# Three down-projection quarters as seven block products with weight sums built by accumulating transfers

## The chip, the cores and the metric

One core of one Trainium2 chip runs the kernel. The metric is the device time of one launch in microseconds (us), over several runs; lower is better. The kernel before has a median of 1753.64 us over 3 runs (1753.59 to 1753.92).

## What is computed

A two-layer decoder trunk over 512 positions with model width 1024, in float32. Each layer normalizes its input, makes one combined projection, runs four attention-like mixers, mixes them through gates and an output projection, and then runs a feed-forward block. The change touches the feed-forward block alone:

```python
for l in range(DEPTH):                      # DEPTH = 2
    ...
    x = x + mixed @ w_out[l]
    h2 = rmsnorm(x, norm2_g[l])
    x = x + jnp.square(jax.nn.relu(h2 @ w_up[l])) @ w_down[l]
return rmsnorm(x, final_g)
```

Here `w_up` is 1024 x 4096 and `w_down` is 4096 x 1024, so the hidden width is 4096.

## The kernel before

**Split products.** TensorE works on fp32r operands. Each fp32 operand is held as a high half (a copy to fp32r) and a low half (the value less its high half), and each product of a 128x128 stationary block with a 128x512 moving block is made by the three matmuls of `mm3` (L288 to L291): high by high, high by low, low by high.

**The weight stream.** All large weights are stored in one array, in the order in which they are used, in pieces of 128 x 2 x 512 (two blocks of 128 rows of the contraction by 512 columns, 512 KB). `weight_plan` (L62) writes that order. `WeightStream` loads a piece into one of three `raw` buffers by a transfer on SP's queue (L105) and splits it: ScalarE (ACT) writes the high half `whi` (L114), VectorE (DVE) the low half `wlo` (L116). The split halves have three buffers each (`wsp`). `next` hands out a piece and issues the splits of the pieces up to two places ahead of it, so a piece's split can start when the piece three places earlier has been used up.

**A large product.** `big` (L293) makes a 512 x 512 result in four PSUM accumulators (`acc`, a pool of four) over eight blocks of the contraction, in four pieces. In each piece it runs over the four accumulators `m` and the two blocks `q`, with one `mm3` each: 24 matmuls a piece, 96 for the result. `evac` then empties each accumulator.

**The feed-forward block.** `up(b)` (L1022) makes 512 of the 4096 hidden rows by `big`, transposed (hidden rows on partitions, 512 tokens in the free dimension), and its `evac` makes relu (L1027), the square (L1029), the high half `ah` (L1032) on ACT and the low half `al` (L1033) on DVE for each 128 rows. `down(c, half)` (L1038) contracts quarter `c` of the hidden rows (1024 of them, eight blocks) with 512 of the 1024 output columns; its `evac` adds the scaled accumulators to the residual `xs` on DVE (L1041). The two are interleaved: while quarter `c` is contracted, the two `up` products of quarter `c + 1` run, in the order up, down, up, down. The last quarter has no `up` beside it. `r2` is the squared reciprocal norm, which is applied at the `evac` of `down`.

```python
        acts = up(0) + up(1)
        for c in range(4):
            nxt = up(2 * c + 2) if c < 3 else []
            for half in range(2):
                down(c, half, acts, finish if l + 1 == DEPTH and c == 3 and half == 1 else None)
                if half == 0 and c < 3:
                    nxt = nxt + up(2 * c + 3)
```

The order on each engine comes from a scheduling layer, which places instructions by what they depend on; within one engine it is then fixed, and an instruction that waits holds those behind it.

Of the kernel before, what the change touches and what calls it, by code (L numbers as in the profile page):

```python
# [8 lines left out]
F32 = mybir.dt.float32  # L9
F32R = mybir.dt.float32r  # L10
# [6 lines left out]
P = 128  # L17
# [43 lines left out]

def weight_plan():  # L62
    plan = []

    def block(layer, key, kt, n):
        for p in range(0, kt, 2):
            plan.append((layer, key, p, min(2, kt - p), n))

    for l in range(DEPTH):
        for b in ("BA", "BF"):  # L70
            block(l, (b,), KD, BA_N if b == "BA" else 512)
        block(l, ("uq",), 2, 384)
        block(l, ("ukv",), 1, 512)
        for b in ("BV", "BD", "BN"):
            block(l, (b,), KD, 512)
        for br in LIFT_ORDER:
            for half in range(2):
                block(l, ("gate", br, half), KD, 512)
                block(l, ("lift", br, half), 2, 512)
        for half in range(2):  # L80
            block(l, ("out", half), KD, 512)
        block(l, ("up", 0), KD, 512)
        block(l, ("up", 1), KD, 512)
        for c in range(4):
            if c < 3:
                block(l, ("up", 2 * c + 2), KD, 512)
            block(l, ("down", c, 0), KD, 512)
            if c < 3:
                block(l, ("up", 2 * c + 3), KD, 512)
            block(l, ("down", c, 1), KD, 512)  # L90
    return plan


class WeightStream:
    def __init__(self, nc, raw, split, wbig, ahead=W_AHEAD, ahead_raw=AHEAD_RAW):
        self.nc, self.raw, self.split, self.wbig = nc, raw, split, wbig
        self.plan = weight_plan()
        self.ahead, self.ahead_raw = ahead, ahead_raw
        self.pos = self.n_dma = self.n_split = 0
        self.raws, self.parts = {}, {}  # L100

    def _dma(self, j):
        _, _, _, kk, n = self.plan[j]
        t = self.raw.tile([P, 2, 512], F32, name="raw", tag="raw")
        self.nc.sync.dma_start(t[:, :kk, :n], self.wbig[j, :, :kk, :n])  # L105
        self.raws[j] = t

    def _split(self, j):
        _, _, _, kk, n = self.plan[j]
        t = self.raws.pop(j)  # L110
        pool, bufs = (self.last_pool, 1) if j == len(self.plan) - 1 else (self.split, 3)
# [3 lines left out]
        eng = self.nc.gpsimd if self.plan[j][1] in ON_POOL and self.plan[j][2] % 4 else self.nc.vector  # L115
        b = eng.tensor_tensor(  # L116
            lo[:, :kk, :n], t[:, :kk, :n], hi[:, :kk, :n].bitcast(F32), op=ALU.subtract)
        self.parts[j] = (hi, lo)
        return a.ins, b.ins
# [7 lines left out]
    def take(self, what):  # L127

        assert self.plan[self.pos][:3] == what
        self.pos += 1  # L130
        return self.parts.pop(self.pos - 1) + self.plan[self.pos - 1][3:]
# [6 lines left out]
    def prefetch(self):  # L138
        last = len(self.plan)
        while self.n_split < min(self.pos + self.ahead, last):  # L140
            while self.n_dma < min(self.n_split + self.ahead_raw, last):
                self._dma(self.n_dma)
                self.n_dma += 1
# [3 lines left out]
    def next(self, layer, key, p):  # L147
# [4 lines left out]
        return self.parts.pop(j) + self.plan[j][3:]  # L152
# [3 lines left out]
def kernel(  # L156
# [53 lines left out]
    tiny([P, 8], "pad", 1)  # L210
# [77 lines left out]
    def mm3(o, ah, al, bh, bl, start, stop):  # L288
        pe.matmul(o, ah, bh, start=start, stop=False)  # L289
        pe.matmul(o, ah, bl, start=False, stop=False)  # L290
        return pe.matmul(o, al, bh, start=False, stop=stop).ins  # L291
# [155 lines left out]
    for l in range(DEPTH):  # L447
# [574 lines left out]
        def up(b):  # L1022
            res = []

            def evac(m, ps):
                t = xp.tile([P, SEQ], F32, name="relu", tag="relu", bufs=3)
                act.activation(t, ps, AF.Relu)  # L1027
                a = xp.tile([P, SEQ], F32, name="sq", tag="sq", bufs=3)
                act.activation(a, t, AF.Square)  # L1029
                hi = xp.tile([P, SEQ], F32R, name="ah", tag="ah", bufs=16)  # L1030
                lo = xp.tile([P, SEQ], F32R, name="al", tag="al", bufs=16)
                act.activation(hi, a, AF.Copy)  # L1032
                dve.tensor_tensor(lo, a, hi.bitcast(F32), ALU.subtract)  # L1033
                res.append((hi, lo))
            big(l, ("up", b), ht, evac, token_stationary=False)
            return res
# [30 lines left out]
        acts = up(0) + up(1)  # L1067
# [4 lines left out]
        for c in range(4):  # L1072
            nxt = up(2 * c + 2) if c < 3 else []
            for half in range(2):
                down(c, half, acts, finish if l + 1 == DEPTH and c == 3 and half == 1 else None)
                if half == 0 and c < 3:
                    nxt = nxt + up(2 * c + 3)
                if c == 3:
                    if l + 1 < DEPTH:
                        htn += norm_half(xs, half, g1, ssq, xp)  # L1080
                        nc.scalar.dma_start(
                            x_dram[l + 1].rearrange("(m p) d -> p m d", p=P)[:, :, half * 512:(half + 1) * 512],
                            xs[half])
                    elif half == 0:
                        sq_half(xs, half, ssq, xp)
                        for m in range(NT):
                            pool.tensor_tensor(xs[0][:, m, :], xs[0][:, m, :], fg[:, 0:512], op=ALU.mult)
            acts = nxt
# [17 lines left out]
def _pack_weights(np, inp):  # L1106
    plan = weight_plan()
# [66 lines left out]
```

## Time and profile before

| | us |
|---|---|
| median of 3 runs | 1753.64 |
| the profiled execution's own time | 1754.36 |
| span of its profile | 1752.6 |
| TensorE (PE) busy in the span | 1730.7 (99%) |
| PE weight loads (PEld) | 1402.9 (80%) |
| DVE busy | 876.2 (50%) |
| ACT busy | 826.2 (47%) |
| GpSimd (POOL) busy | 137.3 (8%) |

The first feed-forward block runs from 529.3 to 879.6 us of the span, the second one ends the program. A matmul's row in the timeline lasts longer than the distance to the next one, since matmuls are pipelined; what one costs in a stream is read from the distance between starts. The profile also gives the granted clock of TensorE in each stretch (PEclk, 1.00 is full).

### The profile page before, as it was taken

To read this page: it belongs to the slowest core of one execution; us is meant where nothing else is said; L and a number is where in the kernel's file an instruction comes from. 1 tells how busy PE (TensorE), PEld (TensorE's weight loads), DVE (VectorE), ACT (ScalarE), POOL (GpSimd) and SP (SyncE) were. 2 spreads that over 40 slices of the span, in tenths; PEclk is the share of its full clock that TensorE was granted. 3 is DMA by queue.
4 is the path that set the end of the run, shared out by engine and by line. 5 is a ranking of instruction groups with operands and counts; after the bars stand their busy time and mean duration, and the time that the engine had idled before them with its cause. 6 is when DMAs were issued, how large, how long until landed. Compare 5 with 4: busy or idle time off the path is not lost.

```text
span 1752.6 us, 22592 instructions
## 1 busy us (share of the span) xinstructions
PE 1730.7 (99%) x8849; PEld 1402.9 (80%) x8849; DVE 876.2 (50%) x1570; ACT 826.2 (47%) x1525; POOL 137.3 (8%) x153
## 2 busy tenths in 40 slices
PE   9999999999999999999999999999999999999998
PEld 7877777778788888888888777777788888888886
DVE  5445999543443333333344479985434433333333
ACT  7576745572334433333346776365623343333332
POOL 2112001011200000000021110011112000000002
PEclk9999999999999999999999999999999999999999
DMA  4222111112242222333332211211124323223322
GB/s 158 96 65 69 61 61 61 61 61 93 88 134 95 97 96 96 96 97 98 115 112 85 72 61 61 83 43 57 61 96 132 108 86 107 96 97 96 96 96 73
DMA packets 50681, 154.07 MB, mean 88 GB/s; under 512 B 5648, under 2 KB 14352, under 8 KB 50576
## 3 DMA queue, kind: packets, MB, share of 16 engines
q1 hardware_dynamic: 48368, 149.41, 26.2%
q10 hardware_dynamic: 2208, 3.23, 0.5%
q8 instruction: 70, 1.15, 0.3%
q14 instruction: 35, 0.29, 0.1%
HBM read 148.43 MB, written 4.19 MB: 87 GB/s over the span
## 4 chain that ended last, share of the span: by engine, by line
PE 86%; DVE 7%; ACT 4%; issue 1%; POOL 0%; POOLq 0%; DVEq 0%; ACTq 0%
PE acc L289 23%; PE acc L291 23%; PE acc L290 23%; PE T L476 3%; PE O L545 2%; PE S L289 2%; DVE wlo L116 2%; PE S L290 2%; PE S L291 2%; ACT whi L114 1%; DVE sc L788 1%; DVE m L787 1%; PE S L487 1%; PE S L488 1%; DVE sc L805 1%
## 5 line engine op out<-in xcount | busy, mean ns | idle before, releaser
L116 DVE TENSOR_TENSOR wlo<-raw,whi 128x1024 fp32r<-128x1024 f32 (+1 forms) x268 | 338.1, 1261 | 556.3 <-ACT whi L114 555.7
L114 ACT ACTIVATE whi<-raw 128x1024 fp32r<-128x1024 f32 (+1 forms) x268 | 281.7, 1051 | 604.2 <-PE acc L291 377.8
L289 PE MATMUL acc<-whi,hth 128*128 128x512 f32 (+1 forms) x960 | 389.1, 405 | 0.0
L290 PE MATMUL acc<-wlo,hth 128*128 128x512 f32 (+1 forms) x960 | 377.2, 393 | 0.5 <-DVE wlo L116 0.5
L291 PE MATMUL acc<-whi,htl 128*128 128x512 f32 (+1 forms) x960 | 377.0, 394 | 0.0
L291 PEld LDWEIGHTS acc<-whi,htl 128*128 128x128 f32 x960 | 180.6, 188 | 35.4
L289 PEld LDWEIGHTS acc<-whi,hth 128*128 128x128 f32 x960 | 181.2, 189 | 33.3 <-issue 2.7
L290 PEld LDWEIGHTS acc<-wlo,hth 128*128 128x128 f32 x960 | 181.1, 189 | 31.3 <-DVE wlo L116 0.8
L289 PE MATMUL acc<-hth,whi 128*128 128x512 f32 x512 | 199.5, 390 | 0.0
L290 PE MATMUL acc<-wlo,ah 128*128 128x512 f32 x512 | 199.4, 389 | 0.0
L289 PE MATMUL acc<-whi,ah 128*128 128x512 f32 x512 | 199.4, 389 | 0.0
L291 PE MATMUL acc<-whi,al 128*128 128x512 f32 x512 | 199.4, 389 | 0.0
L290 PE MATMUL acc<-htl,whi 128*128 128x512 f32 x512 | 199.3, 389 | 0.0
L291 PE MATMUL acc<-hth,wlo 128*128 128x512 f32 x512 | 199.3, 389 | 0.0
L290 PEld LDWEIGHTS acc<-wlo,ah 128*128 128x128 f32 x512 | 96.1, 188 | 20.4 <-DVE wlo L116 0.4
L290 PEld LDWEIGHTS acc<-htl,whi 128*128 128x128 f32 x512 | 96.1, 188 | 20.0
L291 PEld LDWEIGHTS acc<-hth,wlo 128*128 128x128 f32 x512 | 96.1, 188 | 20.0
L289 PEld LDWEIGHTS acc<-whi,ah 128*128 128x128 f32 x512 | 96.1, 188 | 19.8
L291 PEld LDWEIGHTS acc<-whi,al 128*128 128x128 f32 x512 | 96.1, 188 | 19.8
L289 PEld LDWEIGHTS acc<-hth,whi 128*128 128x128 f32 x512 | 96.1, 188 | 19.7
L520 ACT ACTIVATE PT<-T 128x128 f32<-128x128 f32 (+3 forms) x160 | 69.4, 433 | 62.9 <-PE T L476 61.5
L499 DVE TENSOR_REDUCE nm<-S 128x1 f32<-128x128 f32 (+3 forms) x160 | 77.0, 485 | 39.5 <-PE S L497 27.9
(228 smaller groups left out, 2115.7 us busy)
## 6 DMA issues: line engine op xcount, KB each, us to landing
raw<-in_wbig SPq DMA_DIRECT2D x256, 512.0 KB, 3.3
x<-in_x SPq DMA_DIRECT2D x8, 512.0 KB, 5.9
raw<-in_wbig SPq DMA_DIRECT2D x8, 472.0 KB, 4.7
xmid<-x ACTq DMA_DIRECT2D x2, 1024.0 KB, 4.6
x<-xmid SPq DMA_DIRECT2D x4, 512.0 KB, 5.3
ck<-in_cmpk SPq DMA_DIRECT2D x4, 256.0 KB, 4.2
ck<-in_cmpv SPq DMA_DIRECT2D x4, 256.0 KB, 3.7
out<-o ACTq DMA_DIRECT2D x4, 256.0 KB, 2.8
```

Source lines behind the costliest of these rows:

```text
L114: a = self.nc.scalar.activation(hi[:, :kk, :n], t[:, :kk, :n], AF.Copy)
L116: b = eng.tensor_tensor(lo[:, :kk, :n], t[:, :kk, :n], hi[:, :kk, :n].bitcast(F32), op=ALU.subtract)
L289: pe.matmul(o, ah, bh, start=start, stop=False)
L290: pe.matmul(o, ah, bl, start=False, stop=False)
L291: return pe.matmul(o, al, bh, start=False, stop=stop).ins
L476: pe.transpose(t[:width, m * P:(m + 1) * P], s, ident)
L487: pe.matmul(s[:, :n], q[0][:, qc], k[0][:, :n], start=True, stop=False)
L488: pe.matmul(s[:, :n], q[0][:, qc], k[1][:, :n], start=False, stop=False)
L499: dve.tensor_reduce(nm, s[:, :n], axis=AX.X, op=ALU.max, negate=True)
L520: act.activation(pT[:, :n], t[:, :n], AF.Copy)
L545: pe.matmul(o[64 * e:64 * e + 64, P * i:P * (i + 1)], paths[c][2](j, h + e), pTs[e][:, j * P:(j + 1) * P], start=(j == 0 and c == 0 and ex ...
L787: dve.max(m8, a[:, :n])
```

## The change

The first three of the four quarters of the down-projection are written as two-by-two blocks: a quarter's hidden values are `a11`, `a12`, `a21`, `a22` (halves by 512 hidden rows and by 256 tokens) and its weights four blocks of 512 x 512. Instead of eight block products, seven are made (the Winograd form of Strassen's scheme), of sums of blocks on both sides. A block product takes two pieces of weights; a piece is used by two token blocks of 128 instead of four, so it has 12 matmuls instead of 24. A quarter's two `up` products are cut into their eight pieces, and one block product follows each of them from the second on.

- **Sums of hidden blocks.** `up` now writes the squares into one tile `a` per quarter. Four sums of 128 x 4 x 256 are made on DVE (`cmb`), and seven left operands of the same size are split into `ah` and `al`, by seven ACT and seven DVE instructions a quarter.
- **Sums of weights.** Product 1 and product 3 load their blocks as before, but into `sum` buffers. When such a piece has been split, a transfer on POOL's queue with `accum_op=ALU.add` adds the next block of the chain to it in place, out of HBM (products 1, 5, 6, 4 are one chain, 3 and 7 the other): eight accumulating transfers of 512 KB a quarter, 48 in all. The split of the next product's piece waits for it. A quarter now has 22 pieces to split (8 of `up`, 14 of products) where it had 16, and 14 loads on SP's queue.
- **Results.** Products 1, 6, 7 and 4 go on accumulating in one pair of PSUM banks (the two `S` tiles); product 2 takes the tiles `T` and `O`, and products 5 and 3 together take these two again. The feed-forward block otherwise uses these banks only for transposes. After each product both banks are added to `xs` with `r2` or its negative: 14 DVE additions of 128 x 512 a quarter where there were 8.
- **The last quarter** is done as before, from four splits of 128 x 1024.
- Blocks that several products use are stored once; `ON_POOL`, which was empty, is gone; the scratch for software descriptors and one padding tile are larger.

The core of the diff:

```diff
+PRODUCTS = {
+    1: ("a", (0, 0)), 2: (None, (1, 0)), 5: ("a", (0, 1)), 3: ("c", (1, 1)),
+    6: ("a", (1, 1)), 7: ("c", (0, 1)), 4: ("a", (1, 0)),
+}
+ORDER = (1, 2, 5, 3, 6, 7, 4)
+N_SEVEN = 3
...
+    def product(layer, c, i):
+        chain, (kh, nh) = PRODUCTS[i]
+        for q in range(2):
+            src = source(layer, ("down", c, nh), 4 * kh + 2 * q, 2, 512)
+            plan.append((layer, ("seven", c, i), 2 * q, 2, 512, src, chain and (chain, q)))
...
+            if c < N_SEVEN:
+                for j in range(8):
+                    piece(l, steps[j][:2], steps[j][2], KD, 512)
+                    if j:
+                        product(l, c, ORDER[j - 1])
+            else:
+                block(l, ("down", c, 0), KD, 512)
+                block(l, ("down", c, 1), KD, 512)
...
     def _dma(self, j):
+        if chain is None:
+            if self.in_raw == self.ahead_raw:
+                return False
+            self.in_raw += 1
+            t = self.raw.tile([P, 2, 512], F32, name="raw", tag="raw")
+        elif self.plan[j][1][2] in (1, 3):
+            t = self.chains.tile([P, 2, 512], F32, name="sum", tag="sum" + chain[0], bufs=4 if chain[0] == "a" else 2)
+        else:
+            return True
+        self.nc.sync.dma_start(t[:, :kk, :n], self.wbig[src, :, :kk, :n])
...
     def _split(self, j):
...
+        if chain is not None:
+            for i in range(j + 1, min(j + 24, len(self.plan))):
+                if self.plan[i][6] == chain and self.plan[i][1][:2] == self.plan[j][1][:2]:
+                    self.nc.gpsimd.dma_start(t, self.wbig[self.plan[i][5]], accum_op=ALU.add)
+                    self.raws[i] = t
+                    break
...
+        def up_steps(b, a):
...
+                if p == KD - 2:
+                    for m in range(4):
+                        t = xp.tile([P, SEQ], F32, name="relu", tag="relu", bufs=3)
+                        act.activation(t, accs[m], AF.Relu)
+                        act.activation(a[:, 4 * (b % 2) + m, :], t, AF.Square)
+                yield
+
+        def halves(src, shape):
+            hi = xp.tile(shape, F32R, name="ah", tag="ah", bufs=4)
+            lo = xp.tile(shape, F32R, name="al", tag="al", bufs=4)
+            act.activation(hi, src, AF.Copy)
+            dve.tensor_tensor(lo, src, hi.bitcast(F32), ALU.subtract)
+            return hi, lo
+
+        def seven(c, a, between):
+            a11, a12, a21, a22 = a[:, 0:4, 0:256], a[:, 4:8, 0:256], a[:, 0:4, 256:512], a[:, 4:8, 256:512]
...
+            def left(i):
+                if i == 5:
+                    sums[5] = combo()
+                    dve.tensor_tensor(sums[5], a22, a21, ALU.subtract)
+                    sums[7] = combo()
+                    dve.tensor_tensor(sums[7], a11, a21, ALU.subtract)
+                if i == 3:
+                    sums[6] = combo()
+                    dve.scalar_tensor_tensor(sums[6], sums[7], -1.0, a22, ALU.mult, ALU.subtract)
+                    sums[3] = combo()
+                    dve.scalar_tensor_tensor(sums[3], sums[6], -1.0, a12, ALU.mult, ALU.subtract)
+                return halves({1: a11, 2: a12, 4: a22}.get(i, sums.get(i)), [P, 4, 256])
...
+            opens = {1: [ps_s, ps_s], 2: [ps_t, ps_o], 5: [ps_t, ps_o]}
+            bank = {1: 1, 6: 1, 7: 1, 4: 1, 2: 2, 5: 5, 3: 5}
...
+            next(between, None)
+            ready = left(ORDER[0])
+            for n, i in enumerate(ORDER):
+                next(between, None)
+                hi, lo = ready
+                if n < 6:
+                    ready = left(ORDER[n + 1])
+                if i in opens:
+                    banks[i] = [f() for f in opens[i]]
+                bk = banks[bank[i]]
+                for p in (0, 2):
+                    wh, wl, _, _ = ws.next(l, ("seven", c, i), p)
+                    for m in range(2):
+                        cols = slice(m * P, (m + 1) * P)
+                        for q in range(2):
+                            mm3(bk[m], hi[:, p + q, cols], lo[:, p + q, cols], wh[:, q, :], wl[:, q, :],
+                                i in opens and p + q == 0, p + q == 3, i not in opens)
+                add(*where[i][:2], bk, where[i][2])
...
+        for c in range(N_SEVEN):
+            nxt = hidden()
+            seven(c, a, both(c + 1, nxt))
+            a = nxt
+        acts = []
+        for p in range(0, KD, 2):
+            hi, lo = halves(a[:, p:p + 2, :], [P, 2, 512])
+            acts += [(hi[:, q, :], lo[:, q, :]) for q in range(2)]
+        for half in range(2):
+            down(3, half, acts, finish if l + 1 == DEPTH and half == 1 else None)
```

How the engines' instructions stand, at three places (tile names carry buffer numbers; what an instruction waits for is in brackets: PE, Activation, DVE, a transfer of SP or ACT as DMAHW, one of POOL as DMASW).

The first place is PE in the first layer, from the end of the first `up` product of the interleaved part into what follows it. Before, the rest of that `up` product is followed by the first half of the first quarter's `down`:

```order
L289 MATMUL acc_5652<-hth_5312,whi_5688 128x512 [waits Activation_49]
...
L289 MATMUL acc_5808<-whi_5718,ah_5467 128x512 [waits Activation_49]
L290 MATMUL acc_5808<-wlo_5719,ah_5467 128x512 [waits DVE_49]
...
L289 MATMUL acc_5809<-whi_5718,ah_5467 128x512 [waits Activation_49]
```

Now the second `up` piece is followed by product 1 in the banks `S`, the third `up` piece (back in the same `acc`), and product 2 in the banks `T` and `O`:

```order
L336 MATMUL acc_5620<-hth_5140,wlo_5579 128x512 [waits DVE_49]
...
L334 MATMUL S_5692<-whi_5626,ah_5655 128x512 [waits PE_49]
L335 MATMUL S_5692<-wlo_5627,ah_5655 128x512 [waits DVE_49]
...
L334 MATMUL S_5693<-whi_5626,ah_5655 128x512 [waits PE_49]
...
L334 MATMUL S_5692<-whi_5659,ah_5655 128x512 [waits Activation_49]
...
L334 MATMUL acc_5620<-hth_5294,whi_5694 128x512 [waits Activation_49]
...
L334 MATMUL T_5772<-whi_5712,ah_5688 128x512 [waits Activation_49]
...
L334 MATMUL O_5773<-whi_5712,ah_5688 128x512 [waits PE_49]
```

So `up` pieces and block products alternate, in different banks. Over the whole program PE has 8195 matmul instructions where it had 8339.

The second place is POOL in the first layer's feed-forward block. Before, nothing stands between the reciprocal norm and the next layer:

```order
L280 TENSOR_TENSOR r2_5335<-r2_5335,mhalf_89 128x4 [waits DVE_49]
L908 MEMSET vcr_10114 128x256 [waits PE_49]
```

Now the accumulating transfers stand there, each after the split of the piece that it adds to, and ACT's split of the next piece of the chain waits for it, with the next left operand's split and the next `relu` behind. POOL:

```order
L325 TENSOR_TENSOR r2_5335<-r2_5335,mhalf_89 128x4 [waits DVE_49]
L162 DMA sum_5514<-in_wbig 128x1024 [waits DMAHW6_49,DVE_49]
L162 DMA sum_5516<-in_wbig 128x1024 [waits DMAHW7_49,DVE_49]
L162 DMA sum_5514<-in_wbig 128x1024 [waits DMASW0_49,DVE_49]
L162 DMA sum_5516<-in_wbig 128x1024 [waits DMASW1_49,DVE_49]
L162 DMA sum_5732<-in_wbig 128x1024 [waits DMAHW1_49,DVE_49]
```

and ACT:

```order
L155 ACTIVATE whi_5792<-sum_5514 128x1024 [waits DMASW0_49,DVE_49,PE_49]
L1093 ACTIVATE ah_6002<-cmb_5766 128x1024 [waits PE_49]
L155 ACTIVATE whi_5811<-sum_5516 128x1024 [waits DMASW1_49,DVE_49,PE_49]
L1083 ACTIVATE relu_5840<-acc_5620 128x512 [waits PE_49]
```

The buffers `sum_5514` and `sum_5516` are filled once by SP and then added to three times.

The third place is DVE in the first layer, where the last block product ends and the plain last quarter begins. Before, its `al` splits stand among the weight splits, ahead of the additions of the `down` that runs beside them:

```order
L1033 TENSOR_TENSOR al_7217<-sq_7214,ah_7216 128x512 [waits Activation_49]
L116 TENSOR_TENSOR wlo_7235<-raw_7136,whi_7234 128x1024 [waits DVE_49,DMAHW5_49,PE_49,Activation_49]
L1033 TENSOR_TENSOR al_7225<-sq_7222,ah_7224 128x512 [waits Activation_49]
L116 TENSOR_TENSOR wlo_7265<-raw_7166,whi_7264 128x1024 [waits DMAHW6_49,DVE_49,Activation_49]
...
L1041 SCALAR_TENSOR_TENSOR x_4985<-acc_7228,r2_5335,x_4985 128x512 [waits PE_49]
```

Now (`S_6838` and `S_6839` hold product 4):

```order
L156 TENSOR_TENSOR wlo_7259<-sum_6651,whi_7258 128x1024 [waits DMASW7_49,Activation_49]
L1094 TENSOR_TENSOR al_7343<-a_6765,ah_7342 128x1024 [waits Activation_49]
L156 TENSOR_TENSOR wlo_7299<-raw_7152,whi_7298 128x1024 [waits DMAHW1_49,PE_49,Activation_49]
L156 TENSOR_TENSOR wlo_7317<-raw_7170,whi_7316 128x1024 [waits DMAHW2_49,Activation_49]
L1123 SCALAR_TENSOR_TENSOR x_4982<-S_6838,r2_5335,x_4982 128x512 [waits PE_49]
L1123 SCALAR_TENSOR_TENSOR x_4982<-S_6839,r2_5335,x_4982 128x512 [waits PE_49]
L1094 TENSOR_TENSOR al_7347<-a_6765,ah_7346 128x1024 [waits Activation_49]
L156 TENSOR_TENSOR wlo_7357<-raw_7238,whi_7356 128x1024 [waits DMAHW3_49,Activation_49]
```

Of the last quarter's four left splits, three stand ahead of the additions of product 4, and the fourth, which the fourth piece of `down` needs, right behind them.

## Rows read from the trace of the kernel before

**Rows 1.** The page's head: span, and busy time by engine.
```profile
span 1752.6 us, 22592 instructions
PE 1730.7 (99%) x8849; PEld 1402.9 (80%) x8849; DVE 876.2 (50%) x1570; ACT 826.2 (47%) x1525; POOL 137.3 (8%) x153
```

**Rows 2.** The page's chain that ended last, by engine and by line.
```profile
PE 86%; DVE 7%; ACT 4%; issue 1%; POOL 0%; POOLq 0%; DVEq 0%; ACTq 0%
PE acc L289 23%; PE acc L291 23%; PE acc L290 23%; PE T L476 3%; PE O L545 2%; PE S L289 2%; DVE wlo L116 2%; PE S L290 2%; PE S L291 2%; ACT whi L114 1%; DVE sc L788 1%; DVE m L787 1%; PE S L487 1%; PE S L488 1%; DVE sc L805 1%
```

**Rows 3.** Busy time by stretch, four quarters of the first feed-forward block.
```profile
core 0: us, PE busy (x) PEld busy (x) DVE busy (x) ACT busy (x) POOL busy (x), PEclk, DMA share, GB/s
530.00:617.04 87.04, 87.04 (x386) 72.08 (x385) 32.04 (x39) 39.28 (x63) 1.29 (x2) 1.00 0.29 97
617.04:704.08 87.04, 87.04 (x386) 72.10 (x385) 30.62 (x33) 29.84 (x41) 0.00 (x0) 1.00 0.30 97
704.08:791.12 87.04, 87.04 (x386) 72.10 (x385) 30.62 (x33) 29.85 (x41) 0.00 (x0) 1.00 0.31 97
791.12:878.00 86.88, 86.88 (x393) 72.00 (x392) 32.13 (x35) 27.77 (x40) 0.00 (x0) 1.00 0.31 102
```

**Rows 4.** Timeline of PE, 600 to 625 us: start, duration, instruction.
```profile
600.16 0.39 PE L289 MATMUL acc<-whi,ah 128*128 128x512 f32 x1
...
615.80 0.39 PE L289 MATMUL acc<-whi,ah 128*128 128x512 f32 x1
...
616.48 0.39 PE L289 MATMUL acc<-hth,whi 128*128 128x512 f32 x1
...
620.56 0.39 PE L289 MATMUL acc<-hth,whi 128*128 128x512 f32 x1
```

**Rows 5.** Waits in 530 to 878 us, the longest: total, times, longest.
```profile
DVE wlo L116 <- ACT whi L114: 185.1, 64, 4.3
ACT whi L114 <- PE acc L291: 118.1, 31, 4.4
```

**Rows 6.** Waits of SP's queue in the same stretch.
```profile
SPq L105 <- DVE wlo L116: 324.6, 64, 7.2
```

**Rows 7.** Groups by line and shape, 530 to 878 us: busy, mean ns, idle before.
```profile
L116 DVE TENSOR_TENSOR wlo<-raw,whi 128x1024 fp32r<-128x1024 f32 x62 | 76.0, 1226 | 176.6 <-ACT whi L114 176.6
L114 ACT ACTIVATE whi<-raw 128x1024 fp32r<-128x1024 f32 x61 | 64.7, 1060 | 204.6 <-PE acc L291 109.3 <-PE acc L290 95.4
L1033 DVE TENSOR_TENSOR al<-sq,ah 128x512 fp32r<-128x512 f32 x32 | 22.1, 691 | 28.2 <-ACT ah L1032 28.2
L1041 DVE SCALAR_TENSOR_TENSOR x<-acc,r,x 128x512 f32<-128x512 f32 x30 | 21.8, 748 | 7.4 <-PE acc L291 7.4
L1029 ACT ACTIVATE sq<-relu 128x512 f32<-128x512 f32 x32 | 20.1, 629 | 0.5
L1027 ACT ACTIVATE relu<-acc 128x512 f32<-128x512 f32 x32 | 18.8, 587 | 4.2 <-PE acc L291 4.2
```

**Rows 8.** DMA issues over the whole program: count, KB each, median us to landing.
```profile
raw<-in_wbig SPq DMA_DIRECT2D x256, 512.0 KB, 3.3
xmid<-x ACTq DMA_DIRECT2D x2, 1024.0 KB, 4.6
```

**Rows 9.** DMA queues over the whole program: packets, MB, share of 16 engines.
```profile
q1 hardware_dynamic: 48368, 149.41, 26.2%
q10 hardware_dynamic: 2208, 3.23, 0.5%
q8 instruction: 70, 1.15, 0.3%
q14 instruction: 35, 0.29, 0.1%
```

More of the change, by code (lines that the diff above doesn't have):

```diff
@@ L84, in weight_plan @@
         for c in range(4):
[L85 to L91, printed above, removed]
+            steps = [("up", 2 * c + 2 + h, p) for h in range(2) for p in range(0, KD, 2)] if c < 3 else []
+            if c < N_SEVEN:
[6 more added lines that the diff above has]
+                block(l, ("down", c, 1), KD, 512)
+    return blocks, plan
 class WeightStream:
@@ L114, in _split @@
         a = self.nc.scalar.activation(hi[:, :kk, :n], t[:, :kk, :n], AF.Copy)
-        eng = self.nc.gpsimd if self.plan[j][1] in ON_POOL and self.plan[j][2] % 4 else self.nc.vector
-        b = eng.tensor_tensor(
+        b = self.nc.vector.tensor_tensor(
             lo[:, :kk, :n], t[:, :kk, :n], hi[:, :kk, :n].bitcast(F32), op=ALU.subtract)
         self.parts[j] = (hi, lo)
+        if chain is not None:
[4 more added lines that the diff above has]
+                    break
         return a.ins, b.ins
@@ L140, in prefetch @@
         while self.n_split < min(self.pos + self.ahead, last):
-            while self.n_dma < min(self.n_split + self.ahead_raw, last):
-                self._dma(self.n_dma)
+            while self.n_dma < min(self.n_split + 7, last) and self._dma(self.n_dma):
                 self.n_dma += 1
@@ L208 @@
     nc.scalar.dma_start(gains, gains_in)
-    tiny([P, 8], "pad", 1)
+    tiny([P, 32], "pad", 1)
     ws = WeightStream(nc, rawp, wsp, wbig)
@@ L286, in rms, with mm3 @@
         return rsqrt_mean(s, DM, tag)
[L288 to L291, printed above, removed]
+    def mm3(o, ah, al, bh, bl, start, stop, more=False):
+        pe.matmul(o, ah, bh, start=start, stop=False, skip_group_check=more)
+        pe.matmul(o, ah, bl, start=False, stop=False, skip_group_check=more)
+        return pe.matmul(o, al, bh, start=False, stop=stop, skip_group_check=more).ins
     def big(layer, key, xt, evac, kt=KD, token_stationary=True, tick=None, whole=False):
@@ L1019 @@
         dve.tensor_tensor(r2, r2, r2, ALU.mult)
[L1022 to L1036, printed above, removed]
+        nr2 = tiny([P, NT], "nr2", 1)
@@ L1065, in finish, with both @@
             nc.sync.dma_start(ov[m][:, 512:], o)
-        acts = up(0) + up(1)
+        def both(c, a):
+            yield from up_steps(2 * c, a)
+            yield from up_steps(2 * c + 1, a)
+        a = hidden()
+        for _ in both(0, a):
+            pass
         if l + 1 < DEPTH:
@@ L1071 @@
         htn = []
[L1072 to L1088, printed above, removed]
+        for c in range(N_SEVEN):
[3 more added lines that the diff above has]
+        acts = []
+        for p in range(0, KD, 2):
+            hi, lo = halves(a[:, p:p + 2, :], [P, 2, 512])
+            acts += [(hi[:, q, :], lo[:, q, :]) for q in range(2)]
+        for half in range(2):
+            down(3, half, acts, finish if l + 1 == DEPTH and half == 1 else None)
+            if l + 1 < DEPTH:
+                htn += norm_half(xs, half, g1, ssq, xp)
+                nc.scalar.dma_start(
+                    x_dram[l + 1].rearrange("(m p) d -> p m d", p=P)[:, :, half * 512:(half + 1) * 512],
+                    xs[half])
+            elif half == 0:
+                sq_half(xs, half, ssq, xp)
+                for m in range(NT):
+                    pool.tensor_tensor(xs[0][:, m, :], xs[0][:, m, :], fg[:, 0:512], op=ALU.mult)
         ht = htn
```

52 lines of the change are left out of this document (40 added, 12 removed).

## The prediction, made before the changed kernel ran

> **What bounds the kernel now.** I read the page's head first: TensorE is busy for 99% of the span [rows 1]. The chain of waits says the same in another way: 86% of it is PE, and its three longest entries are the three matmuls of `mm3` [rows 2]. An average over stages does not say what an edit in one stage is worth, so I then read the busy time by stretch inside the first feed-forward block [rows 3]: in four stretches of a quarter each, PE is busy for the whole of every one, at a granted clock of 1.00, while DVE is busy for 30.6 to 32.1 us of 87.04 and the transfers take a 0.29 to 0.31 share of the DMA engines. The waits of that stretch confirm it: DVE and ACT wait for the halves and for PE to free a buffer [rows 5], SP's queue waits for DVE to free a `raw` buffer [rows 6], and PE is in no row of the list as a waiter. So this stage is bound by the number of matmuls, and what one costs is the distance between starts. For matmuls with `ah` stationary it is (615.80 - 600.16) / 69 = 0.2267 us, for those of `up` (620.56 - 616.48) / 18 = 0.2267 us [rows 4]. Both kinds cost the same, so a piece with 24 matmuls takes 5.44 us and one with 12 takes 2.72 us.
>
> **What the change removes.** A quarter of the down-projection had two halves of four pieces with 24 matmuls, 192 in all. Seven block products have two pieces with 12 each, 168. That is 24 fewer a quarter, in three quarters and two layers 144, which is also what the two instruction lists differ by (8339 and 8195). The matmuls that stay have the same shape, a 128x128 stationary block and 512 moving columns. 144 x 0.2267 = **32.6 us** come off PE. The `up` matmuls and the last quarter keep their number.
>
> **What it adds, and what covers it.** A quarter now takes 8 x 5.44 + 14 x 2.72 = 81.6 us of PE time; everything added lies on other engines and costs nothing as long as it stays under that and each piece is ready in time.
>
> *DVE.* 22 weight splits and 7 left splits of 128x1024 at 1.226 us [rows 7] are 35.6 us; 14 additions at 0.748 us are 10.5 us; two of the four sums cost as much as a split, the other two, of the additions' kind, 0.748 + (1.226 - 0.691) = 1.28 us, together 5.0 us. That is 51 us of 81.6, where it was 30.6 of 87.04. *ACT.* 22 + 7 copies at 1.060 us and eight times relu and square at 0.587 and 0.629 us [rows 7] are 40.5 us of 81.6. Neither becomes the bound by its sum.
>
> *In time?* The tightest place I find is the first quarter of a layer, where DVE's list has the sums and three left splits crowded ahead of the split of the third `up` piece. Counted from the end of the second `up` product, DVE starts after ACT's first copy at 1.06 us, has ten instructions of 128x1024 (12.4 us), waits once more for ACT's copy of the last sum (1.06 us), and ends that split at about 14.5 us. PE has by then two `up` pieces and product 1 to do (16.32 us), and the low half is first read by the third matmul, at 16.8 us. So 2.3 us are left over. In later quarters the same row has more room, since the hidden values are ready earlier. After a product, its two additions (1.5 us) are in front of the next weight split, and the next user of the same banks comes only after an `up` piece of 5.44 us, so both are covered. At the start of the plain quarter the left splits of the first three pieces stand ahead of product 4's additions, so PE does not wait for these additions; if they stood behind, it would be some 2 x 0.748 + 1.226 = 2.7 us a layer.
>
> *Loads.* SP issues 14 plain loads a quarter where it issued 16, and its queue spent 324.6 us of the 348 us waiting for buffers [rows 6], so it has time to spare. The edits to stored order, padding and scratch move nothing on an engine.
>
> *Accumulating transfers.* These are the one part whose price no row shows: no queue of the page belongs to POOL [rows 9]. The lower bound is a plain 512 KB load, 3.3 us from issue to landing; as upper bound I take three passes one after the other (read HBM, read the buffer, write it), 9.9 us. A transfer of twice the bytes took 4.6 us [rows 8]; that is nearest to two operands of 512 KB, and I take it. What they may take: the next use of a chain's buffer is two products later, that is 4 x 2.72 + 2 x 5.44 = 21.8 us; the split before it takes 2.3 us, so ACT finds the sum ready if the transfer needs less than 19.5 us. PE itself would start to wait about 5.9 us after that, because a piece is split 8.16 us ahead of its use and its split takes 2.3 us. What is queued behind ACT's wait is the next left split and the `relu` that frees `acc`. Even the upper bound of 9.9 us stays under half of 25. By throughput: a plain piece occupies the 16 engines for 0.30 x 87.04 / 16 = 1.63 us [rows 3]; 14 plain ones and 8 at twice that are 49 us of 81.6, a share of 0.60. They would have to cost 4.5 times a plain piece to fill the quarter. POOL's queue has nothing else in this stage that anyone waits for. So I cost them at nothing.
>
> DVE's rows bear on this from another side: the instruction of 128x1024 takes 0.535 us more than that of 128x512 [rows 7], and DVE will be busy for 63% of a quarter. The Trainium skill (page "SBUF — State Buffer", section "Summary: rules for kernel authors") advises against hiding a transfer that is issued from GpSimd under DVE's work, because its descriptors are held up while DVE runs in its two- and four-fold modes, and to issue it from ACT or SP. No row here shows a transfer from POOL, so the trace cannot say whether this bites; the same page (section "Who interferes with whom") gives `tensor_tensor`, which most of these DVE rows are, no such mode. By the row the sum stays at 32.6 us; by the rule, taken at its strongest, it would be the first rival.
>
> **The sum.** Against the profiled execution's 1754.36 us (span 1752.6 [rows 1] and 1.8 around it): 1754.36 - 32.6 = 1721.7 us. That execution lies 0.7 us over the median of the runs shown, so for the median I say **1721.0 us**.
>
> **The rivals.**
>
> *The accumulating transfers become the bound (slower).* If POOL's transfers ran one at a time, eight of them would have to fit in 81.6 us, 10.2 us each. From 10.88 us each (8 x 10.88 = 87.04) a quarter is as long as before the change, and every further microsecond costs 8 x 6 = 48 us: at 12 us the kernel would take about 1754 + 54 = 1807 us. A way to get there: transfers that advance only while DVE is idle, 36% of a quarter, would take 4.6 / 0.36 = 12.8 us, that is 1846 us. For it: no row shows their price, and they read, add and write. Against it: the upper bound from rows is 9.9 us, and POOL's list waits only for the piece's own split and for transfers issued several places earlier, so two can be under way together. Chance 0.05.
>
> *DVE is late at the head of the quarters (a smaller gain).* The sums and left splits read 4 x 256 blocks out of a larger tile instead of one row of 1024. Seven of them stand in that crowded place. If each took 27% longer, the 2.3 us would be gone; at one and a half times (4.3 us more) PE would wait 2 us in each layer's first quarter, 1725 us; at twice (8.6 us more) some 6.3 us there and about 4 us in each of the other four quarters, that is 2 x 6.3 + 4 x 4 = 29 us, 1750 us. For it: 2.3 us is the smallest margin in the chain. Against it: such a block is still read in runs of 256 neighbours, and in these rows the price follows the number of elements [rows 7]. Chance 0.08.
>
> *No gain at all.* PE's matmuls could be as many as before, or wider; the instruction lists exclude both. A change of the granted clock is excluded as long as PE has no gaps; it was 1.00 [rows 3]. What is left of it is some cost that takes back just the 32 us, chance 0.02.
>
> **How the numbers follow.** Forecast 0.85, at 1721 us; its own error is some 2.5 us, from the few waits of under a microsecond that I cannot see at 42 products. The range starts at 1718.5 and goes to 1732, to take in the milder half of the second rival; the worse half and the first rival, less than 2 in 10, are left out. About 0.2% (3.5 us) is what a measurement of this kernel can tell from no change. Faster by more than that: 0.85 + 0.08 = 0.93; within it 0.02; slower 0.05.
>
> **What would show it right or wrong.** Right: in a quarter of the new feed-forward block PE is busy throughout, the block's stretch is 16.3 us shorter in each layer, matmuls still start 0.2267 us apart, DVE is busy for about 51 us of 81.6, the DMA share is near 0.6, and ACT's splits of `sum` tiles wait for PE rather than for a DMASW transfer. Wrong: PE rows that wait for `wlo` or `whi` of a `sum` tile, with ACT waiting for POOL's transfer in front of them (first rival), or for `wlo` of an `up` piece with DVE busy without a break before it (second rival); or accumulating transfers that land later than 19.5 us after issue. A time above 1732 us or below 1718 us would make the prediction wrong.

## The result, and the profile after

| | before | changed kernel |
|---|---|---|
| median of 4 runs each, us | 1753.78 (1753.59 to 1754.28) | 1730.71 (1730.39 to 1731.33) |
| ratio | | 0.9868, 95% interval 0.9851 to 0.9886 |
| span of the profile, us | 1752.6 | 1729.1 |

The kernel became 23.1 us faster. The forecast was 1721.0 us: of the 32.6 us that were worked out, 9.5 are missing, although the time lies inside the range.

The page's head, and the rows on the new transfers, of the changed kernel (they answer to [rows 1, 8, 9]):

```profile
span 1729.1 us, 22542 instructions
PE 1707.2 (99%) x8705; PEld 1376.2 (80%) x8705; DVE 983.5 (57%) x1654; ACT 884.1 (51%) x1547; POOL 179.2 (10%) x201
...
q1 hardware_dynamic: 46640, 143.12, 24.7%
q0 software_dynamic: 6912, 25.17, 8.9%
...
raw<-in_wbig SPq DMA_DIRECT2D x220, 512.0 KB, 3.3
sum<-in_wbig POOLq DMA_DIRECT2D x48, 512.0 KB, 5.4
```

PE has the 144 matmuls less that were counted (8849 and 8705), and is still busy for 99%. The busy time by stretch, the first feed-forward block of the changed kernel (answers to [rows 3]):

```profile
core 0: us, PE busy (x) PEld busy (x) DVE busy (x) ACT busy (x) POOL busy (x), PEclk, DMA share, GB/s
529.00:611.00 82.00, 82.00 (x363) 67.60 (x362) 39.03 (x40) 42.54 (x59) 4.71 (x5) 1.00 0.41 109
611.00:693.00 82.00, 82.00 (x359) 67.09 (x358) 47.83 (x48) 39.29 (x45) 6.99 (x8) 1.00 0.58 139
693.00:775.00 82.00, 82.00 (x358) 67.12 (x357) 48.24 (x47) 38.91 (x45) 7.01 (x8) 1.00 0.55 126
```

The reader sees that the cover held: PE never pauses at a granted clock of 1.00, DVE and ACT have room, and the DMA share is near the 0.6 that was estimated (0.58 and 0.55 in the two stretches that lie wholly among the block products; the first one begins with `up` alone). The waits of this block say the same of the new transfers (engine, line and tile that wait, what they wait for, total, times, longest):

```profile
POOL sum L162 <- DVE wlo L156: 220.0, 21, 40.4
...
ACT whi L155 <- PE S L336: 27.0, 16, 2.0
ACT whi L155 <- PE O L336: 14.2, 9, 2.0
```

There is no row of PE waiting, and none of ACT waiting for an accumulating transfer. So the missing time is not in waits. It is in the matmuls. First the groups of PE by line and shape in that block, then PE's timeline at the two ends of the first half of the plain quarter, 96 matmuls (L334 to L336 are the three lines of `mm3`):

```profile
L334 PE MATMUL acc<-hth,whi 128*128 128x512 f32 x256 | 99.7, 389 | 0.0
L334 PE MATMUL S<-whi,ah 128*128 128x512 f32 x96 | 38.0, 396 | 0.0
L334 PE MATMUL acc<-whi,ah 128*128 128x512 f32 x64 | 25.3, 396 | 0.0
```

```profile
821.10 0.39 PE L334 MATMUL acc<-whi,ah 128*128 128x512 f32 x1
...
843.17 0.40 PE L336 MATMUL acc<-whi,al 128*128 128x512 f32 x1
```

From the first start to the 96th it is (843.17 - 821.10) / 95 = 0.2323 us a matmul, where before it was 0.2267 [rows 4]. Over all 1392 matmuls with `ah` or `al` in the timeline the mean is 0.2328 us, where it was 0.2269 over all of the kernel before. Those of `up` (`hth`, `htl`) went from 0.2268 to 0.2273. 1392 x 5.9 ns + 1536 x 0.5 ns = 9.0 us, nearly all of the missing 9.5. The rise is in the plain quarter too, whose `down` did not change and beside which no transfer accumulates (POOL sends the block's last one at 791.7 us).

What did change there is the **address** of `ah` and `al`. The build gives `whi` and `wlo` (but for the very last piece, which has a pool of its own) addresses that leave 128 on division by 512 in both kernels (bytes in a partition); `ah` and `al` leave 128 before and 256 after. The cause is a line that the prediction passed over: the unused tile `pad` went from 32 to 128 bytes, and `nr2` adds 32, which moves all tiles of the pool behind, `ah` and `al` among them, by 128.

### The profile page after: what moved, and what is told of

The parts are those of the page before. It is cut to its first block, busy times and chain, and to the rows that moved or that the text cites. A ratio compares the mean times of both kernels' runs of the same rounds, so it can differ in the third digit from the quotient of the medians.

```text
span 1729.1 us, 22542 instructions
## 1 busy us (share of the span) xinstructions
PE 1707.2 (99%) x8705; PEld 1376.2 (80%) x8705; DVE 983.5 (57%) x1654; ACT 884.1 (51%) x1547; POOL 179.2 (10%) x201
## 4 chain that ended last, share of the span: by engine, by line
PE 76%; DVE 5%; ACT 2%; issue 1%; POOL 0%; POOLq 0%; ACTq 0%; DVEq 0%
PE acc L336 17%; PE acc L334 17%; PE acc L335 16%; PE S L334 4%; PE S L336 4%; PE S L335 4%; PE T L521 2%; PE O L590 2%; DVE wlo L156 1%; PE T L334 1%; PE O L335 1%; PE O L334 1%; PE T L336 1%; PE O L336 1%; PE T L335 1%
## 5 line engine op out<-in xcount | busy, mean ns | idle before, releaser
L156 DVE TENSOR_TENSOR wlo<-raw,whi 128x1024 fp32r<-128x1024 f32 (+2 forms) x232 | 293.3, 1264 | 418.5 <-ACT whi L155 417.8
L155 ACT ACTIVATE whi<-raw 128x1024 fp32r<-128x1024 f32 (+2 forms) x232 | 243.1, 1048 | 381.6 <-PE acc L336 196.9
L334 PE MATMUL acc<-whi,hth 128*128 128x512 f32 (+1 forms) x960 | 389.0, 405 | 0.0
L336 PE MATMUL acc<-whi,htl 128*128 128x512 f32 (+1 forms) x960 | 377.4, 394 | 0.0
L336 PEld LDWEIGHTS acc<-whi,htl 128*128 128x128 f32 x960 | 180.5, 188 | 35.6
L334 PEld LDWEIGHTS acc<-whi,hth 128*128 128x128 f32 x960 | 181.1, 189 | 33.2 <-issue 2.7
L336 PE MATMUL acc<-hth,wlo 128*128 128x512 f32 x512 | 199.6, 390 | 0.0
L334 PE MATMUL acc<-hth,whi 128*128 128x512 f32 x512 | 199.4, 389 | 0.0
L156 DVE TENSOR_TENSOR wlo<-sum,whi 128x1024 fp32r<-128x1024 f32 x72 | 88.1, 1223 | 64.8 <-ACT whi L155 64.8
L155 ACT ACTIVATE whi<-sum 128x1024 fp32r<-128x1024 f32 x72 | 76.1, 1057 | 90.0 <-PE S L336 43.3
L334 PEld LDWEIGHTS acc<-hth,whi 128*128 128x128 f32 x512 | 96.1, 188 | 20.3
L336 PEld LDWEIGHTS acc<-hth,wlo 128*128 128x128 f32 x512 | 96.1, 188 | 20.0
L708 POOL TENSOR_TENSOR mix<-mix,th 128x512 f32<-128x512 f32 x48 | 63.2, 1328 | 397.7 <-DVE th L707 240.3
L547 ACT ACTIVATE P<-S,nm 128x128 f32<-128x128 f32 (+3 forms) x160 | 83.9, 525 | 22.8 <-DVE nm L544 21.4
L162 POOL DMA_DIRECT2D sum<-in_wbig x48 | 42.1, 877 | 473.0 <-DVE wlo L156 440.5
L334 PE MATMUL S<-whi,ah 128*128 128x512 f32 x192 | 76.0, 396 | 0.0
```

What stands on the lines that cost most here:

```text
L155: a = self.nc.scalar.activation(hi[:, :kk, :n], t[:, :kk, :n], AF.Copy)
L156: b = self.nc.vector.tensor_tensor(lo[:, :kk, :n], t[:, :kk, :n], hi[:, :kk, :n].bitcast(F32), op=ALU.subtract)
L162: self.nc.gpsimd.dma_start(t, self.wbig[self.plan[i][5]], accum_op=ALU.add)
L334: pe.matmul(o, ah, bh, start=start, stop=False, skip_group_check=more)
L336: return pe.matmul(o, al, bh, start=False, stop=stop, skip_group_check=more).ins
L547: act.activation(pt[:, :n], s[:, :n], AF.Exp, bias=nm, accum_out=ls)
```

## The experiments

Two questions: does the address cost the 9 us, rather than the added traffic or the new shape of the tiles; and were the other terms of the sum right, or only untested? Line numbers shift a little from one edited kernel to the next. An expectation calls the three explanations offset, traffic and form theory.

**e1: `ah` back at offset 128.**

```diff
-    tiny([P, 32], "pad", 1)
```

> Edit: the unused tile of 128 bytes at the head of the pool of small tiles is left out, so that every tile of the feed-forward pool (ah, al, sum, cmb) moves down by 128 bytes a partition, and ah and al lie at the same offset within 512 bytes (128) as whi and wlo. Nothing else changes. Offset theory (a matmul whose stationary and moving operand lie at different offsets within 512 bytes starts 5.9 ns later): the 1392 matmuls with ah or al start 0.2267 us apart again, 8.2 us less, with the 0.5 us of up and what attention lost 9 us less, about 1721.5 us. Traffic theory (accumulating transfers and the busier DVE and ACT slow the matmuls): 0.2328 us apart, 1730.7 us. Form theory (tiles of 4 KB read in blocks of 4 x 256): 1730.7 us.

Measured: 1721.54 us, ratio to the kernel before 0.9814 (0.9801 to 0.9828). Its trace shows the same groups and the same 96 matmuls:

```profile
L333 PE MATMUL acc<-hth,whi 128*128 128x512 f32 x256 | 99.7, 389 | 0.0
L333 PE MATMUL S<-whi,ah 128*128 128x512 f32 x96 | 37.3, 389 | 0.0
```

```profile
817.63 0.39 PE L333 MATMUL acc<-whi,ah 128*128 128x512 f32 x1
...
839.16 0.40 PE L335 MATMUL acc<-whi,al 128*128 128x512 f32 x1
```

(839.16 - 817.63) / 95 = 0.2266 us. Leaving out a tile that nothing uses gave 9.2 us, and with it the whole forecast: 1754.12 - 1721.54 = 32.6 us. The added traffic and the new form of the tiles are both still there, so neither of them costs the 9 us.

**e2: the kernel before, moved to offset 256.**

```diff
-    tiny([P, 8], "pad", 1)
+    tiny([P, 40], "pad", 1)
```

> Edit: the kernel before, with its unused small tile grown by 128 bytes, so that ah and al lie at offset 256 within 512 bytes while whi and wlo stay at 128, as in the changed kernel. No block products, no accumulating transfers. Offset theory: its 1536 matmuls with ah or al start 0.2328 us apart, 9.1 us more, and attention loses about 0.5 us as in the changed kernel, about 1763.5 us. Traffic and form theory: unchanged, 1753.8 us.

Measured: 1764.05 us, ratio 1.0056 (1.0043 to 1.0068). It is 9.9 us slower than before. The old kernel, without block products or accumulating transfers, shows the same rise:

```profile
L289 PE MATMUL acc<-hth,whi 128*128 128x512 f32 x256 | 99.8, 390 | 0.0
L289 PE MATMUL acc<-whi,ah 128*128 128x512 f32 x231 | 91.2, 395 | 0.0
```

**e3: no accumulating transfers.**

```diff
-                    self.nc.gpsimd.dma_start(t, self.wbig[self.plan[i][5]], accum_op=ALU.add)
```

> Edit: the changed kernel without its 48 accumulating transfers; a sum tile is split again as it is, so the second to fourth terms of the weight sums are left out of the computation. Offset and form theory: matmuls with ah stay 0.2328 us apart, 1730.7 us, which also says that the transfers are hidden. Traffic theory: spacing falls towards 0.2267 us, as far as 1722 us if the transfers are all of it.

Measured: 1731.28 us, no different from the changed kernel's 1730.71; the mean distance stays 0.2328 us. That is what the offset theory expected, and the 48 transfers cost nothing that this can show.

**e4: is it one operand's address or the pair's?**

```diff
     tiny([P, 32], "pad", 1)
+    rawp.tile([P, 32], F32, name="shift", tag="shift", bufs=1)
+    htp.tile([P, 96], F32, name="shift", tag="shift", bufs=1)
```

> Edit: the changed kernel with 128 bytes put ahead of raw, whi and wlo, and 384 bytes ahead of hth and htl: now whi, wlo, ah and al all lie at offset 256 within 512 bytes, hth and htl at 128 as before. Offset theory, taken of the pair: the 1392 matmuls with ah or al start 0.2267 us apart (8.2 us less), the 1536 of up, which have whi or wlo beside hth or htl, 0.2328 us apart (9.1 us more), and attention's, with the same pair, up to 2700 x 5.9 ns = 16 us more; 1731 to 1748 us. Offset theory, taken of one operand's own place (128 good, 256 bad): both kinds 0.2328 us. Traffic and form theory: ah 0.2328 us, up 0.2267 us, 1730.7 us.

Measured: 1739.55 us, in the middle of the range for the pair. Now the slow ones are `up`'s:

```profile
L336 PE MATMUL acc<-hth,whi 128*128 128x512 f32 x256 | 101.1, 395 | 0.0
...
L336 PE MATMUL S<-whi,ah 128*128 128x512 f32 x96 | 37.4, 390 | 0.0
```

`ah` at 256 is fast when `whi` is at 256 too, and `hth` at 128, fast in every other kernel, is slow beside it. It is the pair. Every edit here moves whole pools, and this run is what ties the cost to a matmul's two operands: `raw`, `whi`, `wlo`, `ah`, `al`, `sum` and `cmb` all stand at 256, only `hth` and `htl` stand elsewhere, and in the block only the matmuls that read these are slow.

**e5 to e7: which distances count?** The edit is the number in `tiny([P, 32], "pad", 1)`: 64, 16 and 8.

> Edit: the changed kernel with its unused small tile grown by 128 bytes, so that ah and al lie at offset 384 within 512 bytes, 256 away from whi and wlo (128). Offset theory, any difference costs the same: 0.2328 us for the matmuls with ah or al, 1730.7 us. Offset theory with a period of 256 bytes: 0.2267 us, 1721.5 us. If a larger difference costs more in proportion (128 bytes: 5.9 ns, 256 bytes: 11.8 ns): 0.2386 us, about 1739 us.

> Edit: the changed kernel with its unused small tile 64 bytes smaller, so that ah and al lie at offset 192 within 512 bytes, 64 away from whi and wlo. Offset theory, any difference costs the same: 0.2328 us, 1730.7 us. With a period of 64 bytes: 0.2267 us, 1721.5 us. In proportion: 0.2297 us, about 1726 us.

> Edit: the changed kernel with the unused small tile of the kernel before (32 bytes), so that ah and al lie at offset 160 within 512 bytes, 32 away from whi and wlo. Offset theory, any difference costs the same: 0.2328 us, 1730.7 us. With a period of 32 bytes: 0.2267 us, 1721.5 us. In proportion: 0.2282 us, about 1724 us.

Measured, with the distance between starts worked out as above from the timeline of the same 96 matmuls of each trace:

| kernel | `ah` less `whi`, bytes within 512 | us between starts | median us |
|---|---|---|---|
| e1 | 0 | 0.2266 | 1721.54 |
| e7 | 32 | 0.2334 | 1731.61 |
| e6 | 64 | 0.2334 | 1731.46 |
| changed kernel | 128 | 0.2323 | 1730.71 |
| e5 | 256 | 0.2267 | 1721.21 |

The rows of the first of these groups, in e5, e6 and e7, agree:

```profile
L334 PE MATMUL S<-whi,ah 128*128 128x512 f32 x96 | 37.4, 389 | 0.0
L334 PE MATMUL S<-whi,ah 128*128 128x512 f32 x96 | 38.0, 396 | 0.0
L334 PE MATMUL S<-whi,ah 128*128 128x512 f32 x96 | 37.9, 395 | 0.0
```

The cost is not in proportion: a distance of 32 costs no less than 128, and 256 costs nothing. Of the distances tried, only those that are multiples of 256 bytes are free. What inside the chip makes it so was not tried and stays open.

**e8: one quarter's block products undone** (from e1).

```diff
-N_SEVEN = 3
+N_SEVEN = 2
...
+        for c in range(N_SEVEN, 3):
+            nxt = hidden()
+            for _ in both(c + 1, nxt):
+                pass
+            acts = whole(a)
+            for half in range(2):
+                down(c, half, acts)
+            a = nxt
```

> Edit: the kernel of e1_offset128 with block products in two quarters instead of three; the third has its eight up pieces first and then its two halves with 24 matmuls a piece. PE has 48 matmuls more. The term of the prediction (a matmul left out is worth 0.2267 us): 48 x 0.2267 = 10.9 us more than e1_offset128's 1721.5 us, 1732.4 us. If part of what the block products take off PE came back as waits, the third quarter gives less: under 10 us, below 1731.5 us. If the plain quarter has waits of its own where its splits are bunched (four of ah and al at once ahead of the weights), above 1733 us.

Measured: 1732.26 us, 10.7 more than e1 for 48 matmuls, where 10.9 was expected. So the main term holds for a single quarter as well.

**e9 and e11: how far is the first rival?** From e1, the accumulating transfer issued twice, and three times.

```diff
                     self.nc.gpsimd.dma_start(t, self.wbig[self.plan[i][5]], accum_op=ALU.add)
+                    self.nc.gpsimd.dma_start(t, self.wbig[self.plan[i][5]], accum_op=ALU.add)
```

> Edit: the kernel of e1_offset128 with each of the 48 accumulating transfers issued twice, one after the other into the same tile; the weight sums then hold their later terms twice, which changes the output. Hidden, as predicted: two take 2 x 5.4 = 10.8 us of the 19.5 us that the chain has, POOL is held 8 x (5.4 + 2 x 0.9) = 58 us of a quarter's 81.6 us, and the 16 engines 14 x 1.6 + 16 x 3.1 = 72 us: no change, 1721.5 us. First rival (transfers from POOL near their limit): PE waits for wlo or whi of sum tiles, some microseconds a quarter, 1730 us or more.

> Edit: as e9_accumulate_twice, with three accumulating transfers in place of one (48 become 144; the output changes). First rival at its price: three in a row into one tile hold POOL 2 x (5.4 + 0.9) + 0.9 = 13.5 us, eight times 108 us of a quarter that has 81.6 us, so six quarters are 26 us longer each, about 1880 us. If POOL does not wait between them, the 16 engines bound it: 14 x 1.6 + 24 x 3.1 = 97 us, 15 us a quarter, about 1813 us. If transfers stay hidden even so: 1721.5 us.

Measured: 1813.65 us and 1881.5 us, ratios 1.0338 (1.0322 to 1.0353) and 1.0726 (1.0705 to 1.0748). The first branch of e9's expectation, hidden as predicted, missed, and of the rival only the direction held: each of six quarters grew by (1813.65 - 1721.54) / 6 = 15.4 us. The traces show POOL's timeline in e1, then in e9, and ACT's in e9 (start, duration, instruction, in brackets the idle time before and what ended it), and then e9's busy time by stretch:

```profile
603.75 0.87 POOL L162 DMA_DIRECT2D sum<-in_wbig  x1 [2.76 <-DVE wlo L156]
...
621.88 0.87 POOL L162 DMA_DIRECT2D sum<-in_wbig  x1 [6.39 <-DVE wlo L156]
```

```profile
605.69 0.86 POOL L163 DMA_DIRECT2D sum<-in_wbig  x1 [4.81 <-DMA sum<-in_wbig]
606.24 1.21 POOL L162 DMA_DIRECT2D sum<-in_wbig  x1
616.85 0.88 POOL L163 DMA_DIRECT2D sum<-in_wbig  x1 [9.40 <-DMA sum<-in_wbig]
617.40 1.23 POOL L162 DMA_DIRECT2D sum<-in_wbig  x1
628.00 0.88 POOL L163 DMA_DIRECT2D sum<-in_wbig  x1 [9.36 <-DMA sum<-in_wbig]
...
638.56 1.23 POOL L162 DMA_DIRECT2D sum<-in_wbig  x1
```

```profile
633.53 1.06 ACT L155 ACTIVATE whi<-sum 128x1024 fp32r<-128x1024 f32 x1 [5.37 <-DMA sum<-in_wbig]
643.64 1.06 ACT L155 ACTIVATE whi<-sum 128x1024 fp32r<-128x1024 f32 x1 [9.05 <-DMA sum<-in_wbig]
```

```profile
602.00:629.00 27.00, 27.00 (x121) 22.36 (x120) 14.32 (x15) 13.70 (x17) 4.54 (x6) 1.00 0.66 135
629.00:684.00 55.00, 42.62 (x165) 33.11 (x164) 21.81 (x22) 16.52 (x20) 6.08 (x7) 0.88 0.69 153
```

The second transfer into a tile waits for the first (L163), and POOL holds the next tile's first behind it. So the second of one tile and the first of the next go out together (605.69 and 606.24), and the next such pair starts 11.2 us later (606.24 to 617.40), not the 7.2 us that the expectation had put together from transfers landing alone in 5.4 us. POOL's queue falls behind: from its fourth sum of the quarter to its seventh it takes 18.1 us in e1 (603.75 to 621.88) and 32.3 us in e9 (606.24 to 638.56). ACT then waits for sums, and PE stands for 12.4 of 55 us. The granted clock is 1.00 while PE has no gaps and 0.88 on average in the stretch where it has them; within it, it falls to 0.50, the lower of its two levels (1.2 GHz), at 643.7 us, in a gap of 3.86 us in which PE waits for ACT's split. Both count: by the heads of the two pages e9's span is 89.0 us longer than e1's, of which 30.1 us are PE busy for longer (1727.8 and 1697.7 us) and the rest is PE standing.

e11's 160 us over e1 is six times 26.7 us, about what its first price, POOL held 108 us a quarter, said. That agreement is luck: PE alone is busy for 59.2 us more there than in e1 (1756.9 us), which the price did not hold, and e9 shows that its parts were not right (transfers that overlap land later).

**e10: DVE's tightest place** (from e1): each of the four sums of hidden values written twice.

```diff
                     dve.tensor_tensor(sums[5], a22, a21, ALU.subtract)
+                    dve.tensor_tensor(sums[5], a22, a21, ALU.subtract)
...
```

> Edit: the kernel of e1_offset128 with each of DVE's four sums of hidden values made twice (same result), four instructions of 128x1024 more in a quarter, all of them ahead of the split of the third up piece. The prediction's tightest place: the split ended 2.9 us before PE needed it in e1_offset128's trace; four instructions that start 1.14 us apart are 4.6 us, so PE waits 1.7 us in the first quarter of each layer, 3.4 us in all, 1725 us; in the later quarters the margin is larger and may hide them. If the margin is larger than read: 1721.5 us. If the place repeats in each quarter: 6 x 1.7 = 10 us, 1731.7 us.

Measured: 1721.65 us, as e1. DVE's timeline around the split in question, of e1 and then of e10:

```profile
584.35 1.23 DVE L1093 TENSOR_TENSOR al<-cmb,ah 128x1024 fp32r<-128x1024 f32 x1 [1.13 <-ACT ah L1092]
585.49 1.22 DVE L156 TENSOR_TENSOR wlo<-raw,whi 128x1024 fp32r<-128x1024 f32 x1
```

```profile
584.39 1.23 DVE L1116 SCALAR_TENSOR_TENSOR cmb<-cmb,a 128x1024 f32<-128x1024 f32 x1
585.53 1.22 DVE L156 TENSOR_TENSOR wlo<-raw,whi 128x1024 fp32r<-128x1024 f32 x1
586.67 1.22 DVE L1118 SCALAR_TENSOR_TENSOR cmb<-cmb,a 128x1024 f32<-128x1024 f32 x1
```

The split starts at the same time: the scheduling layer put part of the doubled work behind it (L1118) and moved the `al` that stood ahead. So this run does not test the margin; it shows only that DVE has room for four more such instructions a quarter. How much later that split could come stays untested.

## Why the prediction was right, and where it was not

*The removed matmuls.* Right in number and, in e1, in value: 32.6 us. The feed-forward block, from the first start of `up` to the last of `down` in the timelines, is 350.0 and 348.4 us in the two layers before, 338.2 and 336.3 us in the changed kernel, 333.7 and 332.0 us in e1. The forecast of 16.3 us a layer is e1's 16.3 and 16.4; the changed kernel has 11.8 and 12.1.

*The step that failed*, a term that stood at nothing, is "The edits to stored order, padding and scratch move nothing on an engine", and with it "The matmuls that stay have the same shape" taken to mean the same price. Same shape was true. But the padding moved `ah` and `al` against `whi` and `wlo`, and the matmuls that stay rose to 0.2328 us: 9.0 us that stood at nothing in the sum. "Matmuls still start 0.2267 us apart" was named as a mark of being right, and it is the mark that failed, and with it the block's stretch that was to be 16.3 us shorter.

That 1730.71 us lies inside the range all the same is luck. The forecast's own error was put at 2.5 us, and it missed by 9.7; the range went up to 1732 us to take in the milder half of the second rival, which did not come true, and the padding's cost happened to fit into that room.

The Trainium skill (page "SBUF — State Buffer", section "Who interferes with whom") gives TensorE separate, independent ports for the moving operand and for the weight load, and lets only the port pair that VectorE and GpSimd share cause contention. Nothing in that rule tells e1 from the changed kernel; they differ by 9.2 us, and the measurement decides. Whether a port has anything to do with it is not shown.

*DVE and ACT.* 51 and 40.5 us a quarter were forecast, 48 and 39 us are in the stretches above. DVE's sum took 1.226 us for each instruction of 128x1024, but back to back they start some 1.14 us apart (584.35 and 585.49 in e1). The second rival's condition did not come up: splits that read 4 x 256 blocks out of a larger tile cost the same as one row of 1024:

```profile
L156 DVE TENSOR_TENSOR wlo<-raw,whi 128x1024 fp32r<-128x1024 f32 x44 | 53.9, 1225 | 106.0 <-ACT whi L155 106.0
...
L1093 DVE TENSOR_TENSOR al<-a,ah 128x1024 fp32r<-128x1024 f32 x13 | 15.9, 1224 | 3.8 <-ACT ah L1092 3.8
```

The 2.3 us of margin at the third `up` piece are 2.9 us in e1: its split ends at 585.49 + 1.22 = 586.71 us, and PE's third matmul of the piece, the first to read it, starts at 589.60.

```profile
589.60 0.39 PE L335 MATMUL acc<-hth,wlo 128*128 128x512 f32 x1
```

*The accumulating transfers.* 4.6 us were taken, 5.4 measured, between the bounds of 3.3 and 9.9, and hidden (e3), although DVE was busy for 48 of 82 us beside them. That one occupies the engines for twice a plain load was a guess that held. In 570 to 780 us of the changed kernel, where 21 of them and 32 plain loads are issued, the queues show:

```profile
q0 software_dynamic: 2922, 10.66, 31.3%
q1 hardware_dynamic: 4608, 16.78, 24.3%
```

By the megabytes in the same rows (512 KB are 0.524 MB) that is 0.313 x 210 x 0.524 / 10.66 = 3.2 us for an accumulating piece against 0.243 x 210 x 0.524 / 16.78 = 1.6 us for a plain one, 2.0 times as much. The Trainium skill (page "Collectives: The Full Stack", section "The bandwidth ceiling: the fold count and why AG ≠ RS ≠ AR") says of transfers between cores that a reduce-scatter runs at about half the rate of an all-gather because its add needs two source reads, with a measured ratio of 1.93. The ratio of 2.0 here, for an add in place, is near it.

But the reserve was judged too well. "They would have to cost 4.5 times a plain piece to fill the quarter" counted bytes alone. Doubled, at 4 plain pieces for each sum, they already made the kernel slower than before (e9), through the order on POOL's queue and landings that take longer when two are under way. e9 puts two transfers in a row, the second of which waits for the first, so it does not say what one transfer of twice the length would cost; it does show that bytes were not the limit that is met first. The rival did not come true here. In its price one number is slipped: with DVE busy for 63% it is idle for 37%, not 36%, which gives 12.4 us a transfer and about 1828 us instead of 1846. No bound of the range hung on it.

## What to carry to other kernels

Count what an edit does to addresses, not only to instructions: a scratch or padding tile that nothing reads can move every pool behind it. In this kernel of back-to-back 128x128 by 512 fp32r matmuls, having the stationary and the moving tile a multiple of 256 bytes apart was worth 5.9 ns in 227 a matmul, or 9 us; e1, the change without its padding tile, beats both kernels. When a bound engine is busy for 99% and yet slower than counted, compare the distance between its starts by tile pair before looking for waits. And a reserve that is counted in bytes says little for a queue that waits in order: double the transfers and see, and mind that the doubling adds a wait of its own.

## What the runs showed of the hardware that was not expected

- The distance between matmul starts depends on where the two operands lie relative to each other: 0.2267 us at 0 or 256 bytes, 0.2323 to 0.2334 us at 32, 64 and 128 (e1, e5 to e7). Moving `whi` and `wlo` beside `ah` and away from `hth` swaps which matmuls are slow (e4).
- PE's busy share and the waits show nothing of it; only the mean of a matmul's row (389 and 395 ns) and the distance between starts do.
- In e9 POOL waits 4.81 us for the landing of an accumulating transfer that it has sent alone, and 9.4 us for one that was sent 0.55 us behind another.
